# A gMLP and latent-attention trunk on one core: row sums ahead of one low part, latent rows copied out of PSUM, two heads in each of two out-projection steps

## The chip, the core and the metric

The kernel runs on one core of a Trainium2 chip. The metric is the device time of one launch in microseconds (us). Two launches' medians that differ by less than about 0.3% (3.4 us here) can't be told apart.

The names of the engines: TensorE is PE, VectorE is DVE, ScalarE is ACT, GpSimd is POOL, SyncE is SP. Matmul results land in PSUM, which has eight banks; everything else lies in SBUF.

## The reference

Two layers on x (256 rows, 2048 columns), float32. Layer one is a gated MLP, layer two is multi-head latent attention with 16 heads. Every sublayer's input is normalised and modulated by a shift and a scale that come from a vector c, and every residual is gated by a vector from c.

```
for each sublayer: shift, scale, gate = silu(c) @ w + b        # 2048 x 6144
h = rms_norm(x) * (1 + scale) + shift
# layer 1
u, v, z = split(h @ w_in, 3)                                   # 2048 x 12288
y = gelu(u) * (w_s . layer_norm(gelu(v)) + b_s) * silu(z);  x += gate * (y @ w_out)
# layer 2
c_kv, k_r = split(h_kv @ w_dkv, [512]);  k, v = rms_norm(c_kv) @ w_ukv
c_q,  z   = split(h @ w_in, [512]);      q    = rms_norm(c_q) @ w_uq
o = softmax(mask(q k^T)) v per head      # rope on 64 of 192 columns of q and k
x += gate * ((o * silu(z)) @ w_out)
```

## The kernel before

**Precision.** Every float32 matmul is made of three: weights and activations are split into a high part (ACT cast, `hi` or `hh`) and the remainder (DVE subtraction, `lo` or `hl`), and hi.hi, hi.lo and lo.hi are added up. `split` does both parts, `rest` the low part alone. A weight load (`raw`, 1 MB) is split in two casts and two subtractions of 128x1024.

**Row sums.** Shift, scale and gate vectors are computed without TensorE: `Ada.step` loads 1 MB of the transposed weights (`araw`) and DVE forms the product with c and its row sums (L222; in the layer-two gate `ga1` each is cut in four pieces of 512 columns). Raw and araw loads share four buffers of 1 MB, and SP issues them in the order of the code; each issue waits for its buffer.

**Steps and banks.** A block of a projection runs over steps `kk`, each with 256 rows of weights, for both chunks t of 128 rows. A block with two pieces of 512 columns collects into four PSUM banks (`pm`); the next block takes the same four in a ring, so its first matmul into a bank waits until the bank's result has been read. All other PSUM tiles of layer two (`px` transposes, `pS` scores, `pT` probabilities) take four further banks in the order of the code.

**Order.** `drive` takes step after step: it prepares the next step's weights, issues the matmuls, then the step's `post`, then pops one entry of the queue `later`. At the end of the attention that queue holds the heads: `attend(h)` issues the scores of head h and the output of head h-1; every second head's output is followed by four transposes into `px` and a split into `ybh`, `ybl`, the left operands of the out-projection. Within an engine a scheduler sorts the instructions when the kernel is built; on the chip each engine then runs its list strictly in that order. Only the opening keeps the order of the code (`nc.keep("order")`); its instructions carry L69 in the profile.

**Places that matter here.** (1) The opening: row sums of the first two 128 columns, the first weights, the first matmuls. (2) The key/value projection `dkv` (two pieces of 288 columns, four banks), whose rows are normalised by `latent_row` straight out of PSUM, and after it the projection to the query latents (`ev_q`), which takes the banks that dkv frees. (3) The out-projection: two blocks i = 0, 1 of eight steps each, `tail=1` (the last step is done bank by bank). In step 3 of block 0 the first half of the gate is requested: `Gate.half` transposes eight columns of `col_ga` on PE, copies them on ACT (`grow`), writes them to memory by a POOL DMA (`gd`) and reads them back to all partitions by a second one (`gate`). `ev_out` then multiplies each bank of the block by the gate on DVE (`res<-pm,gate`), which is what frees the bank.

Of the kernel before, what the change touches and what calls it, by code (L numbers as in the profile page):

```python
# [11 lines left out]
AF = mybir.ActivationFunctionType  # L12
# [11 lines left out]
DR = 64  # L24
# [3 lines left out]
KD = D // P  # L28
# [11 lines left out]
BQ = 0.9  # L40
# [6 lines left out]
START = 2  # L47
# [3 lines left out]
GATE1 = (3, 4)  # L51
FQ = 0.5
ORDER = "zydckkkqqkqkqkqkqkqq"
OQ = 1.0
# [61 lines left out]
def trunk_kernel(ctx: ExitStack, tc: tile.TileContext, a: dict, out: bass.AP):  # L116
    nc = Engines(tc)
# [11 lines left out]
    def slot(name, dtype=F32):  # L129
        return big.tile([P, 2048], dtype, tag="big", name=name)  # L130

    def scratch(shape, name, tag="a", dtype=F32):
        return tmp.tile(shape, dtype, tag=tag, name=name, bufs=SCRATCH[tag])

    def bank(name, tag="aux"):
        return banks.tile(tag, name)
# [9 lines left out]
    col, o = {}, 0  # L146
# [7 lines left out]
    for i in range(4):  # L154
        p = bank("pc", "mm")
# [15 lines left out]
    def squares(dst, src, tag="sq", scale=1.0):  # L171
        j = scratch([P, src.shape[-1]], "sq", tag)
        nc.scalar.activation(j, src, AF.Square, scale=scale, accum_out=dst)

    def rms_rstd(pieces):

        n = len(pieces)
        ss = sml.tile([P, 4], F32, tag="ss4", name="ss4")
        for i, p in enumerate(pieces):
            squares(ss[:, i:i + 1], p, "a")  # L180
        return rstd_sum(ss, n, sum(p.shape[-1] for p in pieces))

    def rstd_sum(ss, n, width):
        if n > 1:
            sq = sml.tile([P, 1], F32, tag="ss1", name="ss1")
            nc.vector.tensor_reduce(out=sq, in_=ss[:, :n], axis=AX.X, op=ALU.add)
        else:
            sq = ss[:, 0:1]
        return rstd_of(sq, 1, 1.0 / width)

    def split(src, hi, lo):
        nc.scalar.copy(hi, src)  # L192
        with behind(chain.pop(0) if chain and queue[0] else None):
            rest(src, hi, lo)

    def rest(src, hi, lo):
        nc.vector.tensor_tensor(out=lo, in0=src, in1=hi.bitcast(F32), op=ALU.subtract)  # L197

    def behind(ins):

        return tc.issue_after(ins.ins) if ins else nullcontext()
# [47 lines left out]
    class Gate:  # L249
# [4 lines left out]
        def piece(self, i):  # L254
            if self.rows is None:
                self.rows = slot("gate")
            g = self.rows[:, i * 512:(i + 1) * 512]
            if i not in self.done:
                self.half(i // 2)
            return g  # L260
# [104 lines left out]
    def load(w, kk, n, nk=2):  # L365
        raw = wraw.tile([P, nk, n], F32, tag="raw", name="raw")
        nc.sync.dma_start(raw, w[kk * P:(kk + 1) * P, :].rearrange("p (c n) -> p c n", n=n))
        return raw
# [27 lines left out]
    later = deque()  # L396
# [178 lines left out]
    def opening(b):  # L575

        ada["sh0"].step()
        ada["sc0"].step()
        raw = load(b.w, 0, b.n)
        wt = [[wsp.tile([P, 1, NB], F32R, tag=g, name=g) for g in ("hi", "lo")] for _ in range(2)]  # L580
        norm0.part(0, h0.at(0, 0))
        nc.scalar.copy(wt[0][0], raw[:, 0:1, :])
        first = nc.scalar.last
        h = scratch([P, S], "h", "h")
        norm0.part(0, h)
        rest(raw[:, 0:1, :], *wt[0])
        norm0.low(h, h0.at(0, 0), h0.at(1, 0))
        split(raw[:, 1:2, :], *wt[1])
        ada["sh0"].step()
        ada["sc0"].step()  # L590
        h = scratch([P, S], "h", "h")
        for dst in (h0.at(0, 1), h):
            norm0.part(1, dst)
        norm0.low(h, h0.at(0, 1), h0.at(1, 1))
        nc.keep("behind")

        def turn(t, q):
            with behind(first):
                norm0.row(t, q, r0[t])
        for q in range(1, 4):  # L600
            for t in range(NT):
                later.append(lambda t=t, q=q: turn(t, q))
        return [(hi[:, 0, :], lo[:, 0, :]) for hi, lo in wt], b.lhs(0)
# [164 lines left out]
    gate1 = Gate("ga1")  # L768
# [23 lines left out]

    def latent_row(pieces):

        r = rms_rstd(pieces)
        cn = scratch([P, R], "cn", "b")
        o = 0
        for p in pieces:
            n = p.shape[-1]
            nc.scalar.activation(cn[:, o:o + n], p, AF.Identity, scale=r)  # L800
            o += n
        return cn

    def latent_turn(which, t, cn, gname):

        p = bank("px", "tr")
        for j in range(4):
            nc.tensor.transpose(p[:, j * P:(j + 1) * P], cn[:, j * P:(j + 1) * P], ident)
        if which not in lat:
            lat[which] = slot("lat" + which, F32R).rearrange("p (w k t) -> p w k t", w=2, t=S)  # L810
        lt = lat[which]
        h = scratch([P, 4, P], "hl")
        for j in range(4):
            nc.vector.tensor_scalar_mul(h[:, j, :], p[:, j * P:(j + 1) * P], col[gname][:, j:j + 1])
        split(h, lt[:, 0, :, t * P:(t + 1) * P], lt[:, 1, :, t * P:(t + 1) * P])

    def z_block(i):
        def ev(t, n, ps):
            if i not in szb:
                szb[i] = slot(f"szb{i}").rearrange("p (t n) -> p t n", t=NT)  # L820
            nc.scalar.activation(piece(szb[i], t, n), ps, AF.Silu)
        return Block(lhs_h1, a["b_w_z"][i], KD // 2, [512, 512], ev)
# [11 lines left out]
    def ev_dkv(t, n, ps):  # L834
        if n == 0:
            half[t] = ps
            return
        w = R - 288
        cn = latent_row([half[t], ps[:, 0:w]])
        kr = ps[:, w:w + DR]  # L840
        r = rms_rstd([kr])
        kn = scratch([P, 1, DR], "kn")
        nc.scalar.activation(kn[:, 0, :], kr, AF.Identity, scale=r)
        if t == 0:
            later.append(lambda: None)
        later.append(lambda: latent_turn("kv", t, cn, "kva"))
        later.append(lambda: rope_key(t, kn))

    def rope_key(t, kn):
        kd = scratch([P, 2, DR], "kd")  # L850
        rope(kd[:, 0:1, :], kn, 1, t, 1)
        nc.vector.tensor_copy(kd[:, 1, :], kd[:, 0, :])
        p = bank("px", "tr")
        nc.tensor.transpose(p[:, :P], kd.rearrange("p a b -> p (a b)"), ident)
        nc.vector.tensor_copy(krT[0:DR, 0, t * P:(t + 1) * P], p[0:DR, :P])
        hold[0] = nc.vector.tensor_copy(krT[DR:, 1, t * P:(t + 1) * P], p[DR:, :P])

    def ev_q(t, n, ps):
        cn = latent_row([ps])
        if t == 0:  # L860
            later.append(lambda: None)
        later.append(lambda: latent_turn("q", t, cn, "qa"))
# [142 lines left out]
    def ev_out(t, n, ps, i):  # L1005
        c0 = i * NB + n * 512
        r = scratch([P, 512], "res")
        residual(r, x1[t][:, c0:c0 + 512], c0, ps, gate1)
        nc.scalar.dma_start(out[t * P:(t + 1) * P, c0:c0 + 512], r)

    def attention():
        b = z_block(1)
        b.first = banks.next
        parts = {
            "z": z_block(0).items(BQ, start=START), "y": b.items(BQ), "d": Block(lhs_k, a["kv_w_dkv"][0], KD // 2, [288, 288], ev_dkv).items(),
            "c": Block(lhs_h1, a["b_w_q"][0], KD // 2, [512], ev_q).items(BQ2)}
        todo = {"q": [queries(i) for i in range(8)], "k": [keys(i) for i in range(8)]}
        for n in ORDER:
            if n in parts:
                yield from parts[n]  # L1020
            else:
                yield todo[n].pop(0)
        for i in range(2):
            b = Block(lambda kk: lambda c, w: yb[kk // 4][w][:, (kk % 4) * 2 + c, :], a["b_w_out"][i], KD // 2, [512, 512], lambda t, n, ps, i=i: ev_out(t, n, ps, i))
            yield from b.items(OQ, tail=1, at_step={GATE1[i]: lambda i=i: gate1.half(i)})

    def everything():
        yield from gmlp()
        yield from attention()
# [48 lines left out]
```

## Time and profile before

| | us |
|---|---|
| median of 3 runs | 1129.98 (1128.75 to 1131.89) |
| profiled execution | 1134.16 |
| its span, first to last instruction | 1132.5 |
| PE busy | 1097.4 (97%) |
| DVE busy | 950.4 (84%) |
| ACT busy | 620.3 (55%) |

The profiled execution lies 4.2 us above the median of the runs; 1.7 us of it are outside the span. PE is busy almost throughout, so a change can gain only in the few places where PE waits or where its clock is lowered, and it loses wherever a new wait of PE appears. All times of the trace below are counted from the first instruction of the span.

### The profile page before, as it was taken

How to read it: one execution, taken by the hardware profiler on the slowest of the kernel's cores; microseconds unless marked ns; L12 is line 12 of the kernel's file. 1: busy time of each engine (PE TensorE's matmuls, PEld its weight loads, DVE VectorE, ACT ScalarE, POOL GpSimd, SP SyncE). 2: the span in 40 equal slices, each digit the busy share in tenths (PEclk: the TensorE clock that was granted, in tenths of full speed). 3: DMA queues.
4: the chain of work that ended last, by engine and by line, in shares of the span. 5: the costliest groups of instructions: out<-in, count | busy, mean ns of one | idle time of the engine just before them, and what ended most of it. 6: DMA issues, size and time to landing. Idle time of an engine off the chain costs nothing.

```text
span 1132.5 us, 14354 instructions
## 1 busy us (share of the span) xinstructions
PE 1097.4 (97%) x5128; PEld 912.6 (81%) x5128; DVE 950.4 (84%) x1375; ACT 620.3 (55%) x1146; POOL 62.2 (5%) x79
## 2 busy tenths in 40 slices
PE   5999999999999999999999999989999999999998
PEld 4877788887888887888888888868889788898876
DVE  5889899988997887897798899869877658779985
ACT  6844444456754435435354455457737579885322
POOL 1000000000310000000000000000000024220000
PEclk9999999999999999999999999999999999999999
DMA  9987889887998988989979989967896645245893
GB/s 384 353 342 291 329 330 364 343 311 282 351 338 300 367 327 318 386 305 342 343 297 353 375 335 375 353 234 288 318 341 224 221 152 194 105 166 215 301 343 128
DMA packets 52328, 340.41 MB, mean 301 GB/s; under 512 B 5888, under 2 KB 6304, under 8 KB 13984
## 3 DMA queue, kind: packets, MB, share of 16 engines
q1 hardware_dynamic: 50400, 335.29, 78.7%
q0 software_dynamic: 704, 2.11, 0.6%
q10 hardware_dynamic: 1152, 2.10, 0.5%
q8 instruction: 40, 0.66, 0.2%
q14 instruction: 32, 0.26, 0.1%
HBM read 337.36 MB, written 2.11 MB: 300 GB/s over the span
## 4 chain that ended last, share of the span: by engine, by line
PE 73%; DVE 11%; DMA 9%; ACT 3%; issue 3%; POOL 0%; SPq 0%; DVEq 0%; ACTq 0%; POOLq 0%
PE pm L392 60%; DMA araw<-in_ada_wT 5%; PE pk L392 4%; DVE lo L197 4%; DVE araw L222 3%; PE pq L392 2%; DMA araw<-in_kv_ada_wT 2%; DMA raw<-in_b_w_z 1%; PE pmix L663 1%; ACT hi L192 1%; PE pS L967 1%; PE pS L968 1%; DVE v L537 1%; PE pt L670 1%; DVE araw L69 1%
## 5 line engine op out<-in xcount | busy, mean ns | idle before, releaser
L192 ACT CAST hi<-raw 128x1024 fp32r<-128x1024 f32 (+2 forms) x372 | 376.3, 1029 | 358.6 <-PE pm L392 238.8
L197 DVE TENSOR_TENSOR lo<-raw,hi 128x1024 fp32r<-128x1024 f32 (+2 forms) x372 | 436.9, 1195 | 60.5 <-ACT hi L192 58.0
L222 DVE CUSTOM_DVE_ANT_0 araw<-araw,s_b,vec 128x2048 f32<-128x2048 f32 (+1 forms) x124 | 265.6, 2142 | 55.1 <-DMA araw<-in_ada_wT 48.4
L392 PE MATMUL pm<-lo,hh 128*128 128x512 f32 x760 | 245.2, 392 | 3.0 <-DVE lo L197 2.9
L392 PE MATMUL pm<-hi,hl 128*128 128x512 f32 x760 | 243.6, 391 | 0.0
L392 PE MATMUL pm<-hi,hh 128*128 128x512 f32 x760 | 238.2, 393 | 2.6 <-DVE u L537 1.2
L392 PEld LDWEIGHTS pm<-hi,hh 128*128 128x128 f32 x760 | 142.1, 188 | 35.5 <-ACT hi L192 2.2
L392 PEld LDWEIGHTS pm<-lo,hh 128*128 128x128 f32 x760 | 141.6, 188 | 35.3 <-DVE lo L197 6.4
L392 PEld LDWEIGHTS pm<-hi,hl 128*128 128x128 f32 x760 | 142.5, 188 | 29.8
L392 PE MATMUL pm<-lo,shi 128*128 128x512 f32 (+1 forms) x320 | 95.0, 373 | 0.0
L392 PE MATMUL pm<-hi,slo 128*128 128x512 f32 (+1 forms) x320 | 93.4, 371 | 0.0
L392 PE MATMUL pm<-hi,shi 128*128 128x512 f32 (+1 forms) x320 | 91.3, 373 | 0.6 <-ACT hi L192 0.6
L392 PEld LDWEIGHTS pm<-hi,shi 128*128 128x128 f32 x320 | 58.2, 188 | 11.3 <-ACT hi L192 0.9
L392 PEld LDWEIGHTS pm<-lo,shi 128*128 128x128 f32 x320 | 58.2, 188 | 10.1 <-DVE lo L197 0.6
L392 PEld LDWEIGHTS pm<-hi,slo 128*128 128x128 f32 x320 | 58.0, 188 | 10.1
L392 PE MATMUL pm<-hi,gh 128*128 128x512 f32 x160 | 52.3, 400 | 3.5 <-ACT cn L800 2.3
L392 PE MATMUL pm<-lo,gh 128*128 128x512 f32 x160 | 52.8, 397 | 0.0
L392 PE MATMUL pm<-hi,gl 128*128 128x512 f32 x160 | 52.6, 397 | 0.0
L192 ACT CAST shi<-yT 128x512 fp32r<-128x512 f32 x32 | 19.8, 622 | 46.1 <-PE pm L392 46.0
L392 PE MATMUL pm<-hi,ybh 128*128 128x512 f32 x128 | 42.9, 398 | 1.4 <-ACT ybh L192 1.4
L392 PE MATMUL pm<-hi,ybl 128*128 128x512 f32 x128 | 43.1, 399 | 0.0
L392 PE MATMUL pm<-lo,ybh 128*128 128x512 f32 x128 | 43.0, 394 | 0.0
(207 smaller groups left out, 1282.3 us busy)
## 6 DMA issues: line engine op xcount, KB each, us to landing
araw<-in_ada_wT SPq DMA_DIRECT2D x96, 1024.0 KB, 6.6
raw<-in_a_w_in SPq DMA_DIRECT2D x96, 1024.0 KB, 6.7
raw<-in_a_w_out SPq DMA_DIRECT2D x32, 1024.0 KB, 6.9
araw<-in_kv_ada_wT SPq DMA_DIRECT2D x32, 1024.0 KB, 7.3
raw<-in_b_w_z SPq DMA_DIRECT2D x16, 1024.0 KB, 7.5
raw<-in_b_w_out SPq DMA_DIRECT2D x16, 1024.0 KB, 6.1
raw<-in_kv_w_ukv SPq DMA_DIRECT2D x8, 1024.0 KB, 4.9
raw<-in_b_w_uq SPq DMA_DIRECT2D x8, 768.0 KB, 4.5
```

Source lines behind the costliest of these rows:

```text
L69: ins = f(*args, **kw)
L192: nc.scalar.copy(hi, src)
L197: nc.vector.tensor_tensor(out=lo, in0=src, in1=hi.bitcast(F32), op=ALU.subtract)
L222: nc.vector.tensor_tensor_reduce(out=t[:, c], in0=t[:, c], in1=s_b[:, c], scale=1.0, scalar=acc, op0=ALU.mult, op1=ALU.add, accum_out=dst)
L392: nc.tensor.matmul(ps[i][:, :widths[i]], lhsT=lt, rhs=rhs[:, offs[i]:offs[i] + widths[i]], start=(first and c == 0 and which == 0 and rhs ...
L537: nc.vector.tensor_tensor(out=p, in0=ps, in1=p, op=ALU.add)
L663: nc.tensor.matmul(pmix[:, j * 256:(j + 1) * 256], lhsT=wsh["T"][:, g, :], rhs=piece(vt[i], t, n)[:, j * 256:(j + 1) * 256], start=True, s ...
L670: nc.tensor.transpose(pt[:, j * P:(j + 1) * P], y[:, j * P:(j + 1) * P], ident)
L967: nc.tensor.matmul(pS[:, c0:c1], lhsT=qT[:, j, t * P:(t + 1) * P], rhs=kT[:, j, 0:nk], start=True, stop=False)
L968: nc.tensor.matmul(pS[:, c0:c1], lhsT=qrT[:, t * P:(t + 1) * P], rhs=krT[:, j, 0:nk], start=False, stop=True)
```

## The change

Three edits. In `opening` the second chunk's high cast stays where it was, and its low part is issued behind the row sums of the second 128 columns. `latent_row` copies the latent rows out of PSUM on DVE without scaling, and a new function `normalise` squares and scales the copy in SBUF on ACT; the dkv block gets `tail=1`. In steps 1 and 2 of the out-projection's block 0 one more entry of `later` is popped.

```
-        split(raw[:, 1:2, :], *wt[1])
+        nc.scalar.copy(wt[1][0], raw[:, 1:2, :])
         ada["sh0"].step()
         ada["sc0"].step()
+        rest(raw[:, 1:2, :], *wt[1])
...
     def latent_row(pieces):
-        r = rms_rstd(pieces)
         cn = scratch([P, R], "cn", "b")
...
-            nc.scalar.activation(cn[:, o:o + n], p, AF.Identity, scale=r)
+            nc.vector.tensor_copy(cn[:, o:o + n], p)
...
+    def normalise(row):
+        nc.scalar.activation(row, row, AF.Identity, scale=rms_rstd([row]))
...
         cn = latent_row([half[t], ps[:, 0:w]])
-        kr = ps[:, w:w + DR]
-        r = rms_rstd([kr])
         kn = scratch([P, 1, DR], "kn")
-        nc.scalar.activation(kn[:, 0, :], kr, AF.Identity, scale=r)
+        nc.vector.tensor_copy(kn[:, 0, :], ps[:, w:w + DR])
+        normalise(cn)
+        normalise(kn[:, 0, :])
...
         cn = latent_row([ps])
+        normalise(cn)
...
-... [288, 288], ev_dkv).items(),
+... [288, 288], ev_dkv).items(tail=1),
...
+        def onward():
+            if later:
+                later.popleft()()
...
-            yield from b.items(OQ, tail=1, at_step={GATE1[i]: lambda i=i: gate1.half(i)})
+            yield from b.items(OQ, tail=1, at_step={GATE1[i]: lambda i=i: gate1.half(i), **({1: onward, 2: onward} if i == 0 else {})})
```

How the instructions of three places stand in the two programs. Numbers at a name are buffer numbers, which differ between the programs.

**Place 1: DVE between dkv and the query latents.** `pm_6638` to `pm_6641` are the four banks of dkv, `lo_...` are low parts of the next weights. Before, DVE only prepares the root of the mean square (`ss1`, `rs0`):

```order
L197 TENSOR_TENSOR lo_7009<-raw_7006,hi_7008 128x1024
L197 TENSOR_TENSOR lo_7042<-raw_7039,hi_7041 128x1024
L186 TENSOR_REDUCE ss1_6965<-ss4_6960 128x1
L167 TENSOR_SCALAR rs0_6967<-ss1_6965 128x1
L197 TENSOR_TENSOR lo_7071<-raw_7068,hi_7070 128x1024
```

After, the copies stand behind the second of the same low parts:

```order
L197 TENSOR_TENSOR lo_7005<-raw_7002,hi_7004 128x1024
L197 TENSOR_TENSOR lo_7038<-raw_7035,hi_7037 128x1024
L800 COPY cn_6948<-pm_6638 128x288
L800 COPY cn_6948<-pm_6639 128x224
L844 COPY kn_6951<-pm_6639 128x64
L800 COPY cn_6981<-pm_6640 128x288
L800 COPY cn_6981<-pm_6641 128x224
L197 TENSOR_TENSOR lo_7067<-raw_7064,hi_7066 128x1024
```

The first bank is now read by the first copy, and no longer by a scaling on ACT; the third low part moved behind five copies.

**Place 2: PE in steps 5 and 6 of the out-projection's block 0.** `pm_...` are the block's four banks, `px<-ident,col_ga1` is the gate's transpose, `px<-ident,szb1` are transposes of two heads' outputs, `pT` a head's output. Before, in step 5 (weights `hi_9207`, `hi_9211`):

```order
L392 MATMUL pm_8916<-hi_9211,ybl1_8655 128x512
L272 MATMUL px_9171<-ident_89,col_ga1_126 8x128
L392 MATMUL pm_8917<-hi_9211,ybl1_8655 128x512
L392 MATMUL pm_8918<-hi_9207,ybh1_8654 128x512
L392 MATMUL pm_8919<-hi_9207,ybh1_8654 128x512
L392 MATMUL pm_8918<-lo_9208,ybh1_8654 128x512
L1002 MATMUL px_9044<-ident_89,szb1_6604 128x128 x2
```

After, in step 6 (weights `hi_9248`, `hi_9252`), behind the last head's output:

```order
L993 MATMUL pT_9107<-pair_8571,pts_9111 128x128
L994 MATMUL pT_9107<-pair_8571,pts_9111 128x128
L392 MATMUL pm_8914<-hi_9248,ybl1_8653 128x512
L392 MATMUL pm_8915<-hi_9248,ybl1_8653 128x512
L1006 MATMUL px_9118<-ident_89,szb1_6604 128x128 x2
L272 MATMUL px_9187<-ident_89,col_ga1_126 8x128
L392 MATMUL pm_8914<-hi_9252,ybh1_8652 128x512
```

The gate's transpose moved from the middle of step 5 into the middle of step 6: behind ten matmuls of that step, the last head's output and the two transposes ahead of it.

**Place 3: DVE at the end of block 0.** `res<-pm,gate` are the multiplications that free the four banks, `araw_9384`/`araw_9431` (before) and `araw_9429` (after) are row sums in pieces, `lo` low parts of block 1's second step. Before:

```order
L222 ISA araw_9431,part_9433<-araw_9431,s_b_94,vec_83 128x512
L222 ISA part_9433 128x1
L707 TENSOR_TENSOR res_9360<-pm_8917,gate_9152 128x512
L708 TENSOR_TENSOR res_9356<-res_9356,x1_0_185 128x512
L707 TENSOR_TENSOR res_9376<-pm_8918,gate_9152 128x512
L222 ISA araw_9431,part_9435<-araw_9431,s_b_94,part_9433 128x512
L222 ISA part_9435 128x1
L707 TENSOR_TENSOR res_9380<-pm_8919,gate_9152 128x512
```

After:

```order
L222 ISA araw_9429,part_9433<-araw_9429,s_b_94,part_9431 128x512
L222 ISA part_9433 128x1
L708 TENSOR_TENSOR res_9354<-pm_8914,gate_9168 128x512
L708 TENSOR_TENSOR res_9358<-pm_8915,gate_9168 128x512
L708 TENSOR_TENSOR res_9374<-pm_8916,gate_9168 128x512
L708 TENSOR_TENSOR res_9378<-pm_8917,gate_9168 128x512
L197 TENSOR_TENSOR lo_9394<-raw_9391,hi_9393 128x1024
```

The multiplication of the first bank, which before stood two sums earlier (it is out of the piece shown), now comes behind the first two pieces of the second row sum, and all four stand together.

## Rows read from the trace of the kernel before

**Rows 1.** The page, part 1: busy time of each engine, its share of the span, and instructions.
```profile
PE 1097.4 (97%) x5128; PEld 912.6 (81%) x5128; DVE 950.4 (84%) x1375; ACT 620.3 (55%) x1146; POOL 62.2 (5%) x79
```

**Rows 2.** The chain of work from 15 to 30 us (start, us, what).
```profile
19.48 1.14 DVE lo L69
20.62 2.26 DVE araw L69
...
25.39 0.61 ACT hh L69
```

**Rows 3.** The timeline of PE from 13 to 27 us (start, us, instruction, idle time before it and what ended it).
```profile
23.92 1.14 PE L293 MATMUL px<-ident,x 128*128 128x128 f32 x8 [0.24 <-ACT xT L295]
...
26.04 0.73 PE L69 MATMUL pm<-hi,hh 128*128 128x512 f32 x2 [0.98 <-ACT hh L69]
```

**Rows 4.** DMA issues of 13.5 to 14 us: KB, us from issue to landing. It is the load that the second of the row sums at place (1) reads.
```profile
araw<-in_ada_wT SPq DMA_DIRECT2D x1, 1024.0 KB, 7.4
```

**Rows 5.** First the busy time of the engines from 26 to 62 us (stretch, length, busy time and count of PE, PE's weight loads, DVE, ACT, POOL, then granted PE clock, DMA share, GB/s). Then from the waits of PE from 62 to 152 us (total, times, longest).
```profile
26.00:62.00 36.00, 35.96 (x162) 29.80 (x163) 29.43 (x31) 27.51 (x43) 0.00 (x0) 1.00 0.89 343
...
PE pm L392 <- DVE u L537: 1.2, 1, 1.2
```

**Rows 6.** The timeline at the end of dkv, 878 to 886 us.
```profile
878.66 0.69 PE L392 MATMUL pm<-hi,slo 128*128 128x288 f32 x4
878.87 1.23 DVE L197 TENSOR_TENSOR lo<-raw,hi 128x1024 fp32r<-128x1024 f32 x1 [0.37 <-ACT hi L192]
...
881.63 0.50 PE L392 MATMUL pm<-hi,gh 128*128 128x512 f32 x1 [2.28 <-ACT cn L800]
```

**Rows 7.** DVE's copies out of PSUM, by form, 860 to 1020 us (count, busy us, mean ns of one).
```profile
L904 DVE COPY pair<-pk 128x256 f32<-128x256 f32 x16 | 6.5, 419 | 0.6 <-ACT sq L173 0.5
L987 DVE COPY pts<-pT 128x384 f32<-128x384 f32 x9 | 5.0, 552 | 0.0
```

**Rows 8.** Stretches as in the first row of rows 5, around three waits of PE: the column before the last two is the granted clock.
```profile
877.60:881.60 4.00, 1.75 (x14) 1.52 (x12) 3.15 (x5) 3.34 (x8) 0.55 (x1) 1.00 0.78 246
881.60:885.60 4.00, 3.97 (x11) 3.12 (x12) 1.11 (x5) 1.91 (x9) 1.10 (x2) 0.57 0.71 279
757.00:761.00 4.00, 1.61 (x9) 1.41 (x10) 2.69 (x7) 3.58 (x11) 0.56 (x1) 0.78 0.00 0
1076.00:1080.00 4.00, 2.60 (x12) 1.92 (x12) 4.00 (x7) 1.46 (x2) 0.00 (x0) 1.00 1.02 406
```

**Rows 9.** The timeline of PE in block 0 of the out-projection, pieces from 1064.8 to 1083.6 us. The first row is the gate's transpose, the second the first matmul of step 6, the next two the last head's output in that step and the matmul behind it, then the first matmul of step 7 and the first of block 1.
```profile
1065.03 0.27 PE L272 MATMUL px<-ident,col_ga 128*8 128x128 f32 x1
...
1070.26 0.62 PE L392 MATMUL pm<-hi,ybh 128*128 128x512 f32 x2
...
1073.67 0.38 PE L988 MATMUL pT<-pair,pts 128*128 128x128 f32 x2
...
1074.26 0.71 PE L392 MATMUL pm<-hi,ybh 128*128 128x512 f32 x2
...
1077.51 0.50 PE L392 MATMUL pm<-hi,ybh 128*128 128x512 f32 x1 [1.40 <-ACT ybh L192]
...
1083.17 0.39 PE L392 MATMUL pm<-hi,ybh 128*128 128x512 f32 x1
```

**Rows 10.** The chain of work from 1060 us to the end (start, us, what).
```profile
1077.51 28.49 PE pm L392 x124
```

**Rows 11.** The timeline of POOL, 1065 to 1072 us: the two DMAs of the gate.
```profile
1065.88 0.57 POOL L276 DMA_DIRECT2D gd<-grow  x1 [38.97 <-ACT grow L274]
1071.23 0.56 POOL L277 DMA_DIRECT2D gate<-gd  x1 [4.77 <-DMA gd<-grow]
```

**Rows 12.** DMA issues: KB each, median us from issue to landing. The first two rows are the gate's of 1060 to 1090 us; the next is a weight load issued at 1073 to 1074, the next two are loads issued from 1075 to 1083; the next two are the second half of the same gate (1100 to 1120 us); the last two are layer one's gate (618 to 625 us).
```profile
gate<-gd POOLq DMA_DIRECT2D x1, 512.0 KB, 5.9
gd<-grow POOLq DMA_DIRECT2D x1, 4.0 KB, 4.8
...
raw<-in_b_w_out SPq DMA_DIRECT2D x1, 1024.0 KB, 5.9
...
araw<-in_ada_wT SPq DMA_DIRECT2D x2, 1024.0 KB, 6.5
raw<-in_b_w_out SPq DMA_DIRECT2D x1, 1024.0 KB, 7.4
...
gate<-gd POOLq DMA_DIRECT2D x1, 512.0 KB, 3.7
gd<-grow POOLq DMA_DIRECT2D x1, 4.0 KB, 4.0
...
gate<-gd POOLq DMA_DIRECT2D x1, 512.0 KB, 7.9
gd<-grow POOLq DMA_DIRECT2D x2, 4.0 KB, 6.7
```

**Rows 13.** Stretches as in rows 5: the last column but one is the DMA share.
```profile
1065.90:1070.70 4.80, 4.80 (x28) 4.11 (x27) 4.01 (x11) 2.69 (x3) 0.55 (x1) 1.00 0.78 294
1074.20:1079.20 5.00, 3.60 (x18) 2.78 (x17) 4.87 (x11) 2.25 (x3) 0.00 (x0) 1.00 1.01 405
```

**Rows 14.** The timeline of DVE at the end of block 0, 1079 to 1087 us. The first row is the first piece of the row sum that stands ahead of the four multiplications after the change, the second one of these multiplications.
```profile
1082.21 0.75 DVE L222 CUSTOM_DVE_ANT_0 araw<-araw,s_b,vec 128x512 f32<-128x512 f32 x1
...
1082.89 0.69 DVE L707 TENSOR_TENSOR res<-pm,gate 128x512 f32<-128x512 f32 x1
```

More of the change, by code (lines that the diff above doesn't have):

```diff
@@ L1014, in attention @@
         parts = {
-            "z": z_block(0).items(BQ, start=START), "y": b.items(BQ), "d": Block(lhs_k, a["kv_w_dkv"][0], KD // 2, [288, 288], ev_dkv).items(),
+            "z": z_block(0).items(BQ, start=START), "y": b.items(BQ), "d": Block(lhs_k, a["kv_w_dkv"][0], KD // 2, [288, 288], ev_dkv).items(tail=1),
             "c": Block(lhs_h1, a["b_w_q"][0], KD // 2, [512], ev_q).items(BQ2)}
```

## Prediction

> **What bounds the kernel.** I read busy time first: PE is at work for 1097.4 of 1132.5 us [rows 1]. So I went on to PE's waits and to the stretches in which its granted clock falls, and only then to what the change does to those. The profiled execution took 1134.16 us, 4.2 more than the median of the runs; the differences below are worked out in its trace and laid on the median.
>
> Three waits matter. In the opening PE waits 0.98 for the activation of the second chunk [rows 3]; ahead of it stand, on DVE, the second chunk's low part and two row sums of 2.26 [rows 2]. At the end of dkv PE waits 2.28 for ACT's scaling, which must empty the first bank [rows 6], and after that wait the granted clock falls from 1.00 to 0.57, so that 11 PE instructions fit in a stretch of 4 us [rows 8]: half of the two levels, 1.2 instead of 2.4 GHz, for most of it. Before step 7 of the out-projection's block 0 PE waits 1.40 for the cast of the last heads [rows 9]; there the clock stays at 1.00 [rows 8]. From 1077.51 on, matmuls follow each other without a pause: one piece of 28.49 us with 124 matmuls, 0.23 each [rows 10]. Whatever makes PE wait there is added to the end.
>
> **Row sums first.** The low part took 1.14 on the path [rows 2]. Without it the two sums start at 19.48 and 21.74; the second one's data were issued by 14.0 at the latest and took 7.4, so they are there at 21.4 [rows 4]. The activation would start at 24.25 instead of 25.39 [rows 2], but PE is busy with transposes until 23.92 + 1.14 = 25.06 [rows 3]. PE starts at 25.06 instead of 26.04: 0.98 less, not 1.14. The low part then runs from about 24.2 to 25.4 and is read after four matmuls, at 25.06 + 4 x 0.23 = 25.98; hidden. How much survives is the question. From 26 to 62 us PE is busy 35.96 of 36.00 and DVE 29.43 [rows 5], so PE leads and DVE has 6.6 us to follow it; behind 62 PE waits for DVE here and there, 1.2 for `u` [rows 5], and a PE that is early waits longer there. The next weights' load takes the buffer that is now freed by a sum, about 1.1 later; the same 6.6 us cover it. **-0.7**, between 0 (all given back) and -0.98.
>
> **Latent rows.** The first bank of dkv is now freed by the first copy. It stands behind the low part of 878.87 [rows 6]; such a part holds DVE's path for 1.14 [rows 2], so the copy starts at 880.01. A copy of 256 columns takes 0.42 and one of 384 takes 0.55 [rows 7], so 288 take 0.45. The bank is free at 880.46, and with 0.1 for the signal PE starts at 880.56 instead of 881.63 [rows 6]: **-1.07**. PE's wait is then 1.2 instead of 2.28. That lies below the 1.40 after which the clock stayed at 1.00 and far from the 2.28 after which it fell [rows 8]. I take it to stay, and the 4 us at 0.57 cost 4.0 x 0.43 = **-1.7**. If the clock falls nevertheless, this term is nothing. The copies are paid by DVE: per chunk 0.45 + 0.39 + 0.28 at dkv and about 0.7 for the query row, some 3.6 us in all. Queued behind them is the third low part, which comes 1.2 later than before; PE reads it no earlier than after two steps of twelve matmuls, 24 x 0.23 = 5.5 us behind its start. Squares and scalings on the copies come later than before, but the rows are read only by transposes that the new order puts into the middle of the next block. Were that cover gone, its price would be the old wait, 2.28.
>
> **Two heads in each of two steps.** They bring nothing at step 7: the last transposes still stand right ahead of it, and on ACT their cast stays behind the two casts of the next block, so the 1.40 stays. What they do is to push the gate back. Its transpose was at 1065.03 [rows 9]. In the new order it stands behind ten matmuls of step 6, whose first was at 1070.26, behind the last head's output and two transposes: 1070.26 + 10 x 0.227 + (1074.26 - 1073.67) + 0.22 = 1073.34, on the clock of before [rows 9]. From the transpose the chain to the gate is: 0.85 to the first DMA's issue, its transit, 0.54 to the second's issue (1071.23 against 1065.88 + 4.81), its transit [rows 11, 12]. Before, that gave 1077.1, ahead of the first multiplication.
>
> What are the two transits now? In their own rows 4.8 and 5.9, in a stretch with a DMA share of 0.78; where they go now the share is 1.01 [rows 13]. Loads issued there took 5.9 (at the first one's time) and 7.4, 6.5, 6.5, on average 6.8 (at the second one's time) [rows 12]. I take these: 1073.34 + 0.85 + 5.9 + 0.54 + 6.8 = 1087.4. The Trainium skill (DMA: Bandwidth & Descriptors, Anatomy of one DMA) gives a DMA a fixed part of about 2.0 us and then 436 GB/s, which I estimate at 2.0 and 3.2 us for these two; no load here in a full stretch agrees with that, and by it the sum would be that of the rival of the punctual gate below. The first multiplication needs 0.7 [rows 14], so the bank is free at 1088.1. PE would need it at 1083.17 [rows 9]: **+4.9**. Bounds: with the second half's transits, 4.0 and 3.7 [rows 12], the gate is there at 1082.4, but DVE has two sum pieces to do first, from 1082.21 on [rows 14], so the bank is free at 1084.3: +1.1. With layer one's, 6.7 and 7.9 [rows 12], it is 1090.0: +6.9.
>
> Queued behind the waiting multiplications on DVE are the low parts of block 1's second step; PE reads those 28 matmuls into the block, 6.4 us, and they follow 2.4 us after the gate, so PE waits once. The wait is longer than the 2.28 after which the clock fell, so I add the same **+1.7**. The Trainium skill (TensorE: Matmul & The Clock Gate, Part 1: The HAM clock gate) says that the clock has just these two levels and that the window over which activity is judged runs freely and does not start with the kernel, so that two equal waits need not end alike; by that the 1.7 is only likely.
>
> **Sum.** -0.7 - 1.07 - 1.7 + 4.9 + 1.7 = +3.1 us; on the median 1129.98 + 3.1 = 1133.1. That is 0.28% more, just inside the 0.3% (3.4 us) that a measurement of this kernel can tell from no change.
>
> **Rivals.**
> - The gate's transits stay as they were, 4.8 and 5.9: bank free at 1086.1, +2.9, and the sum is +1.1, 1131.1. For it speaks that they are its own rows; against it the share of 1.01.
> - A punctual gate: with the lower transits the wait is 1.1, too short for the clock, and the sum is -2.4, 1127.6; with the whole 0.98 of the opening -2.6. It decides where the chain of two DMAs takes less than 9 us. Against it: the four DMAs of these kinds in busy stretches took 4.8 to 7.9 each. To be faster by over 0.3% it would need no wait for the gate at all, which DVE's order excludes, unless the opening or the clock elsewhere gives 1 us more.
> - The gate is as late as layer one's, +6.9, and the rest as forecast: +5.1, 1135.1, clearly slower.
> - The copies don't keep the clock up (+1.7 on the forecast: 1134.8), or the opening gives all back (+0.7: 1133.8). Either makes it slower by over 0.3%. For the first speaks only that the gap stays.
> - The clock is not lowered behind the wait for the gate: +1.4, 1131.4.
>
> **Chances.** Forecast with its neighbours of up to 0.7 us: 0.30. Own transits: 0.17. Clock not lowered there: 0.13. Punctual gate: 0.10. Late gate: 0.14. Clock falls at dkv, or the opening gives back: 0.16. The forecast's own part below 3.4 is about half of it and a bit more. So within 0.3%: 0.17 + 0.13 + 0.18 = 0.48; slower: 0.12 + 0.14 + 0.16 = 0.42; faster 0.10, the punctual gate with more help. The range goes from 1127.4, just below the punctual gate, to 1136.5, above the late gate; it leaves out less than 2 in 10: a punctual gate with help elsewhere, and a late gate together with a lowered clock at dkv.
>
> **What would show it.** Right: PE starts its second chunk near 25.1; the wait at the end of dkv is near 1.2 and the stretch behind it has a clock of 1.00; a wait of PE of 3 to 6 us at the start of block 1, ended by DVE's multiplication, which itself waited for the gate's DMA; behind it a stretch at half clock; the 1.4 ahead of step 7 unchanged. Wrong: no wait there, or one that a row sum ends; a gate that lands less than 9 us after its transpose; waits for `u` and `lo` between 62 and 152 us that grow by more than 1 us; a half clock behind dkv.

## The result, and the profile after

The changed kernel took 1136.1 us (median; 1133.1 to 1138.5) beside 1132.4 us of the kernel before on the same chip: ratio 1.0039, interval 1.0027 to 1.0050, so 4.4 us slower (3.1 to 5.7). The forecast was +3.1, just inside the 0.3% that can be told from no change; it came out just beyond. Here 1132.4 is the median of 20 runs and the 1129.98 that the forecast was laid on that of three, so it is the differences that are compared, +3.1 forecast and +4.4 measured. Laid on 1129.98, +4.4 is 1134.4, inside the range; 1136.1 lies in it too, at its edge.

Busy time (answers [rows 1]) did not move on PE; DVE has 4.8 us more, where 3.6 were worked out for the copies.

```profile
PE 1097.3 (97%) x5128; PEld 914.9 (80%) x5128; DVE 955.2 (84%) x1381; ACT 621.2 (55%) x1140; POOL 61.5 (5%) x79
```

**Opening.** The timeline of PE, 13 to 27 us, answers [rows 3]: PE's wait for `hh` is 0.23, where it was 0.98.

```profile
25.36 1.20 PE L69 MATMUL pm<-hi,hh 128*128 128x512 f32 x4 [0.23 <-ACT hh L69]
```

Then, from the chain of 55 to 90 us, what PE follows there (start, us, what), the wait in PE's timeline, and the stretch behind it, with columns as in [rows 5]:

```profile
58.95 8.54 DMA araw<-in_ada_wT
...
69.90 7.98 DMA raw<-in_a_w_in
...
77.98 1.05 ACT hi L192
```
```profile
79.08 0.93 PE L392 MATMUL pm<-hi,hh 128*128 128x512 f32 x2 [3.47 <-ACT hi L192]
```
```profile
79.00:83.00 4.00, 3.92 (x10) 3.14 (x11) 2.70 (x3) 1.88 (x4) 0.00 (x0) 0.57 1.01 397
```

Two things are to be seen. PE starts its second chunk early, as forecast: its matmuls are 0.7 us ahead of those of before at 28 us. Then, from 75.6 us on, it waits 3.47 for a weight load that took 7.98, and the stretch behind it has a granted clock of 0.57; at 84 us the matmuls are 4.3 us behind those of before. Whether the edit does this is the question of the first experiments.

**dkv.** The end of dkv, answers [rows 6]: the low part, the two copies of the first chunk, and PE's first matmul into the freed bank. The row under it is the stretch around that wait, and answers the first two of [rows 8].

```profile
878.34 1.23 DVE L197 TENSOR_TENSOR lo<-raw,hi 128x1024 fp32r<-128x1024 f32 x1 [0.36 <-ACT hi L192]
879.48 0.75 DVE L800 COPY cn<-pm 128x288 f32<-128x288 f32 x2
...
879.99 0.50 PE L392 MATMUL pm<-hi,gh 128*128 128x512 f32 x1 [1.17 <-DVE cn L800]
```
```profile
878.50:882.50 4.00, 2.83 (x14) 2.17 (x13) 3.97 (x11) 2.74 (x8) 0.01 (x1) 1.00 0.87 278
```

(The copies' row gives the form of the first one alone.) The wait is 1.17 (2.28 before), the clock stays at 1.00. Counted by the same matmul in the two traces, PE is 0.53 ahead at 858 us and 3.28 ahead at 892: 2.75 gained in this stretch.

**Gate.** From 1060 us on: the waits of PE; the chain from the gate's transpose to the end, in order; PE's first matmul of block 1 and DVE's multiplications in the timeline.

```profile
PE pm L392 <- DVE res L708: 5.1, 1, 5.1
PE pm L392 <- ACT ybh L192: 1.4, 1, 1.4
```
```profile
1069.57 0.12 PE px L272
...
1070.26 4.70 DMA gd<-grow
...
1075.51 9.03 DMA gate<-gd
...
1084.63 0.70 DVE res L708
...
1085.38 24.11 PE pm L392 x96
```
```profile
1079.90 0.39 PE L392 MATMUL pm<-hi,ybl 128*128 128x512 f32 x1
1085.38 0.80 PE L392 MATMUL pm<-hi,ybh 128*128 128x512 f32 x1 [5.09 <-DVE res L708]
```
```profile
1084.63 2.48 DVE L708 TENSOR_TENSOR res<-pm,gate 128x512 f32<-128x512 f32 x4 [3.91 <-DMA gate<-gd]
```
```profile
1082.00:1086.00 4.00, 0.62 (x2) 0.53 (x3) 1.37 (x3) 0.00 (x0) 0.00 (x0) 0.62 0.75 298
1086.00:1090.00 4.00, 4.00 (x11) 3.13 (x10) 4.00 (x7) 0.00 (x0) 0.00 (x0) 0.53 0.01 2
```

The gate lands at 1084.54; DVE had stood idle for it 3.91, PE 5.09. The matmul before the wait began at 1079.90 and one takes 0.23, so PE should have gone on at 1080.13: 5.25 lost. Behind the wait the clock is 0.53, and 96 matmuls take 24.11 where [rows 10] give 96 x 28.49 / 124 = 22.06: 2.05 more. Together 7.3; the matmuls of the two traces give 7.4 (3.05 ahead at 1080 us, 4.39 behind at 1089). The wait ahead of step 7 is 1.4, as in [rows 9]. The two 1 MB loads that were issued 0.2 and 3.1 us behind the gate's second DMA took 8.65 and 8.24.

### The profile page after: what moved, and what is told of

Read it like the earlier page. It is cut to its first block, busy times and chain, and to the rows that moved or that the text cites. A ratio compares the mean times of both kernels' runs of the same rounds, so it can differ in the third digit from the quotient of the medians.

```text
span 1136.8 us, 14359 instructions
## 1 busy us (share of the span) xinstructions
PE 1097.3 (97%) x5128; PEld 914.9 (80%) x5128; DVE 955.2 (84%) x1381; ACT 621.2 (55%) x1140; POOL 61.5 (5%) x79
## 4 chain that ended last, share of the span: by engine, by line
PE 81%; DMA 8%; DVE 6%; issue 2%; ACT 2%; POOL 0%; SPq 0%; DVEq 0%; ACTq 0%; POOLq 0%
PE pm L392 68%; DMA araw<-in_ada_wT 5%; PE pk L392 4%; PE pq L392 2%; DVE lo L197 2%; DVE araw L222 2%; PE pmix L664 1%; DMA raw<-in_a_w_in 1%; ACT hi L192 1%; PE pS L971 1%; PE pS L972 1%; DVE araw L69 1%; DMA gate<-gd 1%; DMA x<-in_x 1%; PE pt L671 1%
```

## Experiments

Two theories stand against each other. The forecast's: the late gate is the loss, the copies gain 2.8 and the opening a little. The rival: the wait near 75 us belongs to the opening edit and is the loss, or the heads cost by themselves through the work that they bring to DVE and ACT.

**The opening alone**, the first diff of the section on the change and nothing else.

> Only the opening's edit. Theory: the row sum that now frees a weight buffer 1.1 us later starts a backlog of the loads, and PE waits 2 to 4 us for a weight cast between 70 and 80 us, more than the 0.7 to 1.0 us it gained at 25 us; PE is 2 to 4 us later than before at 130 us. Later waits of before (1.7 at 267, 1.0 at 449) take most of it back, so the end is within 1 us of before. Rival: the long wait of the changed kernel was a disturbed transfer of one execution; then PE is 0.7 to 1.0 us early at 130 us and the end is 0.7 us earlier than before.

1130.0 us beside 1130.3: ratio 1.0001 (0.9987 to 1.0016). No wait of 3 us near 75, though the sums stand ahead of the low part; the waits of PE from 62 to 152 us (answer [rows 5]) are

```profile
PE pm L392 <- DVE v L537: 1.2, 1, 1.2
PE pm L392 <- ACT hi L192: 0.8, 2, 0.5
PE pm L392 <- DVE lo L197: 0.7, 2, 0.4
PE pm L392 <- DVE u L537: 0.6, 1, 0.6
```

In the trace of before the waits of this stretch come to 3.5 us (the row in [rows 5] is one of them), here, with two small ones that are not shown, to 4.1. Neither theory is borne out: PE does not wait 2 to 4 us near 75, but it isn't 0.7 to 1.0 early at 130 us either, but 0.25 late. Two things are in this. In this execution the gain at the start was only 0.32 at 28 us, for the clock stayed half until later (0.77 from 22 to 26 us, 1.00 before); and what was gained is waited for behind 62 us, as the prediction said it might be. At dkv this kernel, with the old wait of 2.28, has the half clock (0.57 from 880 to 884 us).

**The copies alone**, without the bank-by-bank last step of dkv.

```
-            nc.scalar.activation(cn[:, o:o + n], p, AF.Identity, scale=r)
+            nc.vector.tensor_copy(cn[:, o:o + n], p)
...      (kn likewise; normalise(...) on the copies; items() of dkv as before)
```

> Only the copies of the latent rows, without the tail of the dkv block. Theory: PE's wait behind dkv falls from 2.28 to 1.2 us and the granted clock stays at 1.00 behind it, so PE is 2.7 to 2.8 us early from 892 us to the end: 2.8 us faster. Rival: the tail is what shortens the wait; then the wait stays above 2 us and the time is that of before.

1128.1 us, ratio 0.9982 (0.9968 to 0.9997): 2.0 faster. PE's wait and the stretch around it:

```profile
878.04 0.50 PE L392 MATMUL pm<-hi,gh 128*128 128x512 f32 x1 [1.17 <-DVE cn L799]
```
```profile
876.00:880.00 4.00, 2.83 (x16) 2.26 (x15) 3.63 (x8) 2.98 (x8) 0.00 (x0) 1.00 0.85 292
```

From 858 to 892 us PE gains 2.7 on before. The wait is the same 1.17 as in the changed kernel, so the bank-by-bank last step has no part in it. And this kernel, whose opening is that of before, has the wait near 75 us, with half clock behind it (0.57 from 79 to 83 us):

```profile
79.44 1.20 PE L392 MATMUL pm<-hi,hh 128*128 128x512 f32 x2 [3.20 <-ACT hi L192]
```

So that wait does not need the opening edit. It goes with the load issued near 70 us. Its row (KB, us from issue to landing) in the kernel with the opening alone, in this one, and in the changed kernel:

```profile
raw<-in_a_w_in SPq DMA_DIRECT2D x1, 1024.0 KB, 5.0
```
```profile
raw<-in_a_w_in SPq DMA_DIRECT2D x1, 1024.0 KB, 7.7
```
```profile
raw<-in_a_w_in SPq DMA_DIRECT2D x1, 1024.0 KB, 8.0
```

Over all thirteen traces of this document PE waits 1.9 us or more there in two of the four with the opening edit (3.47 and 1.95) and in three of the nine without it (3.20, 3.04 and 2.47): the load takes 6.5 to 8.0 in these five and 4.7 to 5.1 in the others. So few can't tell whether the edit makes the long one likelier. Since the opening alone takes the time of before, it brings neither a loss nor a gain that can be measured.

The copies alone were run once more beside the last version below:

> The latent-row copies alone once more, on one chip with the version that has the nine idle matmuls. Theory 'the copies are worth 2.0 to 2.8': ratio near 0.998, no half clock behind dkv.

1127.8 beside 1130.4: 0.9977 (0.9963 to 0.9991), 2.6 faster, and no half clock behind dkv. In its trace the wait near 75 us is there too, 3.04, but the clock stays at 1.00 behind it:

```profile
78.65 0.73 PE L392 MATMUL pm<-hi,hh 128*128 128x512 f32 x2 [3.04 <-ACT hi L192]
```
```profile
78.60:82.60 4.00, 3.95 (x17) 3.30 (x18) 2.96 (x4) 2.92 (x5) 0.00 (x0) 1.00 1.00 389
```

**Opening and copies**, no heads moved.

> Row sums ahead of the low part, and the latent rows by copies; no heads moved, no bank-by-bank last step of dkv. Theory 'the copies give 2.0 to 2.7, the opening nothing': 1.5 to 3 us faster than before, wait at the end of dkv near 1.2, no half clock behind it, gate in time. Rival 'the opening gives its 0.7 too once the wait at dkv is gone': 2.7 to 3.5 faster. Rival 'the opening brings the wait near 75 us that the changed kernel showed': a wait of 3 us or more near 75 us, and no faster than before by more than 1.5.

1129.3 beside 1130.6: 0.9983 (0.9968 to 0.9998), 1.9 faster, what the copies give alone. The medians and the trace fit the first theory (wait at dkv 1.2, no half clock behind it, gate in time); the interval, 0.2 to 3.6 us faster, leaves room for the second. In this execution PE waits 1.95 near 75 us, and the stretch from 60 to 85 us cost it 2.9 us against before. The third theory asked for 3 us or more there and a gain of 1.5 at most; neither came.

**The heads alone.**

> Only the two heads in each of two steps. Theory: the gate's transpose stands in step 6, its two DMAs end late, and PE waits 5 to 5.5 us for the first multiplication at the start of block 1; behind the wait the clock is halved for 3.4 to 6.8 us, 1.7 to 2.2 us more: 7 to 7.5 us slower than before. Rival: DVE is what is late (it runs the same work closer together); then the wait is ended by a row sum and is about 1 to 2 us, and the time is 1 to 3 us above before.

1136.3 us, ratio 1.0061 (1.0038 to 1.0084): 6.9 slower. The wait and the clock around the start of block 1:

```profile
1082.92 0.80 PE L392 MATMUL pm<-hi,ybh 128*128 128x512 f32 x1 [5.54 <-DVE res L707]
```
```profile
1082.90:1086.90 4.00, 3.98 (x9) 3.14 (x10) 4.00 (x7) 0.00 (x0) 0.00 (x0) 0.50 0.01 4
```

PE loses 8.2 us there by its matmuls. Ahead of that wait the heads cost PE nothing: it is 5.90 us ahead of before at 1020 us and 5.96 at 1082. The whole loss of the change is in this edit.

The same trace shows something about dkv, which this edit leaves as it was. PE waits the old 2.28 there, and this time the clock does not fall behind it:

```profile
877.38 0.50 PE L392 MATMUL pm<-hi,gh 128*128 128x512 f32 x1 [2.28 <-ACT cn L800]
```
```profile
877.40:881.40 4.00, 4.00 (x18) 3.27 (x19) 1.06 (x5) 1.91 (x9) 1.09 (x2) 1.00 0.86 247
```

**The late gate alone.** The heads stay; the kernel before asks for the gate one step later.

```
-GATE1 = (3, 4)
+GATE1 = (4, 4)
```

> The kernel before with one number changed: the first half of the gate is requested one step later (step 4 of the block instead of 3), the heads stay where they were. In the new order the gate's transpose stands in the middle of step 6, behind the two transposes of that step's heads, as after the change. Theory 'the late gate is the loss': PE waits 4 to 6 us at the start of block 1, ended by DVE's multiplication that waited for the gate's DMA; behind it some 6.8 us at half clock; 6 to 8 us slower than before. Rival 'the heads themselves cost' (they load DVE and ACT earlier and so delay weights): with the heads unmoved a wait of 1 to 3 us at most and less than 3 us slower.

1141.3 beside 1130.6: 1.0083 (1.0052 to 1.0114), 9.4 slower, more than the 6 to 8 expected and far from the rival's 3 (interval 5.9 to 12.9):

```profile
PE pm L392 <- DVE res L707: 6.8, 1, 6.8
```
```profile
gate<-gd POOLq DMA_DIRECT2D x1, 512.0 KB, 9.8
```
```profile
1091.00:1095.00 4.00, 3.21 (x8) 2.54 (x9) 4.00 (x10) 0.00 (x0) 0.00 (x0) 0.50 0.47 199
```

With no head moved, a gate that is asked for at the same place among step 6's matmuls costs as much and more. With the trace of the heads alone, where the heads cost PE nothing ahead of the wait, the moved heads are the loss because they push the gate back; their own work on DVE and ACT isn't needed to explain it. One thing differs from the expectation: here the first multiplication stands behind two pieces of a row sum, whose load landed at 1089.55 and which end at 1091.12, while the gate landed at 1090.02. So what ends this wait is the row sum; by the gate alone it would have been some 0.9 us shorter (an estimate: the multiplication could have begun at 1090.1 and not at 1091.05). That PE waits for the gate's DMA itself is shown by the changed kernel, where DVE stands idle for `gate<-gd`, and by the heads alone, whose chain runs through both of the gate's DMAs to the multiplication.

**The gate asked for first**, with all three edits.

```
+  at_step={1: lambda: (gate1.half(0), onward()), 2: onward}      (block 0; half 1 as before)
```

> The changed kernel, but in step 1 of block 0 the gate's first half is requested ahead of the heads that this step pops, not in step 3. Theory: its transpose stands in step 3 or 4, the DMAs end some 10 us ahead of the multiplications, PE waits for nothing at the start of block 1 and the clock stays: 7 to 7.5 us faster than the changed kernel, 2.5 to 3.5 us faster than before. Rival (DVE late): the wait at the start of block 1 stays at 3 us or more.

1133.5 us, ratio 1.0024 (1.0007 to 1.0042): 2.7 slower than before, where 2.5 to 3.5 faster was expected. The wait at block 1 is gone, and another has come ahead of it, inside block 0, ended by a cast of the heads that stands behind a late weight load; waits from 1040 us on, the chain of that place, and the clock:

```profile
PE pm L392 <- ACT ybh L192: 4.7, 2, 3.3
```
```profile
1052.94 0.52 DVE szb L997 x2
...
1053.85 0.68 DVE ybl L197
...
1054.60 0.65 DVE araw L222
1055.24 0.02 DVE col_ga L222
1055.26 0.02 issue
1055.28 8.37 DMA raw<-in_b_w_out
...
1065.74 0.49 ACT ybh L192
...
1066.28 3.78 PE pm L392 x8
```
```profile
1066.70:1070.70 4.00, 4.00 (x12) 3.24 (x12) 3.62 (x10) 0.00 (x0) 0.00 (x0) 0.50 0.52 190
```

PE loses 7.2 us between 1020 and 1080 us. The load was issued when a row sum for the gate (`col_ga`) gave its buffer back at 1055.26. `Gate.half` asks first for the eight row sums that it needs, so an early gate pulls these sums ahead, and ahead of the last one DVE had the heads' work (`szb`, `ybl` and others) to do. Which of the two delays the buffer isn't told apart.

**Is the half clock the wait's doing?** First the heads alone, and 22 matmuls on PE into an unread bank between the two blocks:

```
+        if i == 0 and t == 1 and n == 1:
+            for k in range(22):
+                ... nc.tensor.matmul(p, lhsT=yb[1][0][:, 0, 0:P], rhs=(512 columns of the same), ...)
```

> The two heads in each of two steps alone, and on PE 22 matmuls of 512 columns between the last matmul of block 0 and the first of block 1, into a bank that nobody reads: 22 x 0.227 = 5.0 us of work in the place of the wait for the gate. Nothing in the result depends on them. Theory 'a wait of that length lowers the clock': the wait shrinks to less than 1.5 us, the clock stays at 1.00 behind it, and the kernel takes 2 to 3.4 us less than with the heads alone (some +4 to +5 against before instead of +6.9). Rival 'the clock has other reasons, or the filling delays as much as it saves': half clock also here, and +6.5 or more against before.

In the trace, the theory: the filling and the first stretch of block 1 are both at a clock of 1.00, and the filling ends 0.3 us behind the multiplication that frees the bank.

```profile
1079.00:1083.90 4.90, 4.90 (x23) 3.98 (x22) 1.32 (x4) 1.49 (x2) 0.00 (x0) 1.00 0.94 368
1084.00:1088.00 4.00, 4.00 (x19) 3.31 (x19) 4.00 (x8) 0.00 (x0) 0.00 (x0) 1.00 0.04 16
```

Up to 1089 us PE loses the 5.0 of the filling here, against 8.2 with the heads alone: 3.2 less. By time it is 1136.4 beside 1130.6, ratio 1.0056 (1.0035 to 1.0077), +6.3 (4.0 to 8.7), an interval that holds +4.5 as well as +6.9; the time doesn't decide, and the trace shows a new wait near 1102 us that costs PE 0.9, behind a row sum's load of 9.50.

The same at dkv, in the kernel before, where the order of every other instruction stays:

> The kernel before, and on PE nine matmuls of 512 columns between the last matmul of dkv and the first of the projection to the query latents, into a bank that nobody reads: 9 x 0.227 = 2.04 us of work in the place of the wait of 2.28; the order of every other instruction is that of before. ACT still scales the latent rows out of PSUM, so the bank comes free as late as before. It measures the second half of the term for the latent rows by itself. Theory 'the clock falls because PE stands still': a wait of about 0.3 is left, no half clock behind it, and PE is 1.5 to 1.8 us earlier at 892 us than before: 0.5 to 2.5 us faster by time. Rival 'the clock falls at that place whatever PE does': half clock as before, no gain.

```profile
876.85 2.22 PE L840 MATMUL px<-gh 128*128 128x512 f32 x9
879.29 0.50 PE L393 MATMUL pm<-hi,gh 128*128 128x512 f32 x1 [0.22 <-ACT cn L801]
```
```profile
880.80:884.80 4.00, 4.00 (x21) 3.34 (x20) 1.29 (x7) 1.97 (x9) 1.00 (x2) 1.00 0.40 159
```

21 instructions in four microseconds instead of the 11 of [rows 8], and from 858 to 892 us PE gains 1.58: nearly the forecast's -1.7, by itself and with the bank no earlier. By time 1129.8 beside 1131.6, 0.9988 (0.9973 to 1.0004), 1.4 faster: in the expected band but not apart from nothing. Since the clock stayed up once behind the unfilled wait as well (the heads alone), this one trace would not decide; the places taken together do. Of the eleven traces with the wait of 2.1 near 758 us unfilled, the clock fell there in all eleven, and in neither of the two with that wait filled (below).

**Can it be carried further?** The copies alone, and nine idle matmuls near 758 us, where PE waits 2.1 for the root of the mean square:

> The latent-row copies alone, and nine idle matmuls at the end of layer one, in the place of PE's wait of 2.12 us for the root of the mean square near 758 us, behind which every kernel so far showed 6.83 us at half clock. Theory 'filled waits keep the clock': no half clock near 758, and 1.5 to 2.5 us less than the copies alone, so 3.5 to 4.5 us faster than before. Rival 'the other short waits there (0.26, 0.57 and 0.81) are enough to lower it, or the rest of the path at that place is ACT's and gives nothing for a faster PE': as the copies alone, 2.0 us faster.

```profile
756.50:760.50 4.00, 2.58 (x12) 2.10 (x13) 3.38 (x10) 2.84 (x9) 0.55 (x1) 1.00 0.01 4
```
```profile
757.92 0.73 PE L393 MATMUL pm<-hi,gh 128*128 128x512 f32 x2 [1.85 <-ACT gh L342]
```

The clock stays at 1.00 (0.78 before, third of [rows 8]), and PE then waits 1.85 for ACT. By time 1127.3 beside 1131.6, 0.9964 (0.9948 to 0.9979). Since from 695 to 858 us its trace gains no more on before than that of the copies alone (2.0 and 1.9), the two were run on one chip:

> The copies and the nine idle matmuls near 758 us once more, beside the copies alone on the same chip. Theory 'the idle matmuls give 1.5 to 2.5': ratio near 0.9964 and 1.5 us or more below the copies alone. Rival 'the path there is ACT's, and the clock that is kept is given back in the wait for gh': within 0.5 us of the copies alone, and from 695 to 858 us PE gains no more than the 1.9 us that the copies alone show in that stretch.

1128.3, against before 0.9985 (0.9972 to 0.9998), 1.7 faster; the copies' 1127.8 on that chip were 2.6 faster. So the lead of the first run did not come again, and no gain of the idle matmuls is shown; the intervals are too wide to exclude one of about 1 us. PE's wait for ACT's `gh`, 0.81 before, is 1.85 with the clock kept, so a part of what the clock gives is waited away. The traces leave open how much: from 695 to 858 us PE gains 2.0 and 2.2 with the idle matmuls, and 1.9 and 0.5 in the two traces of the copies alone. What beats both kernels by time, twice, is the copies alone: some 2.3 us under before, and so, with the +4.4, about 6.7 under the changed kernel (a sum of medians from different chips, an estimate).

## Why the prediction came out as it did

**Sum.** The single edits measured +0.1, -2.0 and -2.6, and +6.9; with the mean of the copies' two, +4.7, and the change as a whole +4.4. The edits add up within their intervals of 1.5 us or more to either side. The forecast had -0.7, -2.8 and +6.6. Its mechanisms were those of the trace. What failed is the sizes: the opening's -0.7 measured nothing, the copies' -2.8 came as -2.3, the gate's +6.6 as +6.9 by time and +7.3 in the changed kernel's trace. Each is off by 0.3 to 0.8 and all to the same side, which took the sum across 0.3%. By time no single term is shown to be off, for each lies in its edit's interval; that the opening gave nothing and the gate more rests on the traces.

**Row sums first: the step that was mis-sized.** PE's wait fell by 0.75, where 0.98 was worked out. "How much survives" was put at 0.7 us; by time the edit alone measured +0.1 (interval -1.5 to +1.8, which holds -0.7 too). In its trace the waits for `v`, `u`, `hi` and `lo` behind 62 us, taken together, grew from 2.7 to 3.3: the one for `u` shrank, and one of 1.2 for `v` came. The 6.6 us of DVE's slack in [rows 5] is an average over 36 us. It does not say that DVE is early at the one instruction for which PE waits next. That the gain is given back there is seen in single traces, and not shown by time.

**Latent rows: right in the mechanism; the clock's part is not there every time.** The first chunk's two copies take 0.75 behind the low part (0.45 + 0.39 worked out), the wait is 1.17 (1.2 taken), the clock 1.00, the gain 2.75 in the trace (2.77 taken); the wait of 1.2 was taken not to lower the clock since 1.40 had not. It didn't in any of the seven traces that have the copies. By time 2.0 and 2.6. In the trace the filling at dkv gives 1.58 by the clock alone. But the forecast took the whole 1.7 as saved, and behind the old wait of 2.28 the clock fell in four traces of five (before, opening alone, late gate alone, 22 matmuls between the blocks) and not in the heads alone. An estimate from these five, 1.07 + 0.8 x 1.7 = 2.4, lies nearer to the time than 2.77 does.

**Step 7: right.** The 1.40 is unchanged, for the reason given.

**The gate: right in its mechanism, low in both terms.** The transits were taken as 5.9 and 6.8 and were 4.70 and 9.03: the sum was off by 1.0 (12.7 against 13.7), the parts by more. The 4 KB took less than the 1 MB load issued 0.2 us ahead of it (5.85). The half megabyte took 8.3 to 9.8 in the four traces with a late gate, and the 1 MB loads issued with it or up to 3.1 us behind it 7.8 to 9.1: it is held up about as they are, but the prediction read the loads of before, 5.9 to 7.4, and in the new order these are slower too (8.65 and 8.24 in the changed kernel). The gate's transpose came 0.7 earlier than worked out, counted on the clock of before, so that the wait was 5.25 and not 4.9; that these two errors nearly cancel is luck. The Trainium skill (DMA: Bandwidth & Descriptors, Anatomy of one DMA) would give 2.0 and 3.2 by estimate; the measurement decides, and in a stream with a share of about 1.0 that formula is no guide.

**The clock behind the gate.** Taken from dkv as 1.7, it was 2.05: here the clock was already half at 1085.38, where PE went on, and 0.53 from 1086 to 1090, against 0.57 over four microseconds at dkv [rows 8]. That it falls at all behind a long wait is likely and not certain: it fell behind this one in the three traces that have it (5.09, 5.54 and 6.78), but not behind the 2.28 of dkv in the heads alone, nor behind the 3.04 near 75 us in the second trace of the copies. The Trainium skill (TensorE: Matmul & The Clock Gate, Part 1: The HAM clock gate) has two levels, and no row here needs a third: 0.53 or 0.57 is the mean of a stretch in which the clock changed.

**Chances.** "Within 0.3%" and "slower" stood at 0.48 and 0.42 with the number at 0.28%. By these chances the side on which it fell was close to even. The rival nearest to what came is the one with the opening given back, +3.8, together with a gate somewhat later.

## What to carry to other kernels

Before work is moved on an engine that runs its list in order, look at what stands behind it: here two heads, which cost PE nothing ahead of the place, pushed a tiny transpose back by one step, and two chained DMAs behind it turned that into 5 us of wait and 2 us lost to the half clock. Request what is on a chain of small DMAs early enough for its transits under load, 14 us here, but count also what the request pulls ahead of the engine that feeds the weights. Where a bank's reader is late, as ACT was here, another engine can copy the bank out and the scaling can follow from SBUF; a wait that this shortens pays twice if the clock fell behind it and no longer does.

## What was not expected of the hardware

- The same 1 MB load near 70 us lands after 4.7 to 5.1 us in eight of the thirteen traces and after 6.5 to 8.0 in five. With the long one PE waits 1.95 to 3.5. The kernel before (4.8) and the copies alone (7.7) have the same instructions up to dkv, so the program is not the reason.
- A wait does not lower the clock each time: behind the same 2.28 at dkv it fell in four traces and stayed at 1.00 in a fifth, and behind a wait of 3.04 near 75 us it stayed, where the waits of 1.95, 2.47, 3.20 and 3.47 at that place in four other traces had half clock behind them.
- Matmuls that nobody reads kept the granted clock at 1.00 in all four traces that have them: 9 of them in a wait of 2.28 gave PE 1.58 back in the trace, 22 in a wait of 5.5 gave 3.2. By time neither gain is apart from nothing, and near 758 us, where ACT's chain is next, none is shown.
- A 512 KB read to all partitions took 8.3 to 9.8 us under a DMA share near 1.0, as long as the 1 MB loads issued with it or behind it (7.8 to 9.1).
